# Seven products instead of eight in one more weight unit of v, with its sums of tokens formed earlier and one group's softmax scaled on ScalarE

## The chip, the cores and the metric

One core of a Trainium2 chip runs the whole program. The metric is the device time of one execution in microseconds (us), as the median of several runs; lower is better. PE stands for TensorE's matmuls, DVE for VectorE, ACT for ScalarE, POOL for GpSimd, SP for the engine that issues most transfers.

## The reference

Two layers work on 256 tokens of 2048 features. Layer 0 mixes by causal pooling, layer 1 by attention; each mixer is followed by a gated feed-forward part, with a layer norm behind every step. The change lies in layer 1. There, q, k and v are three products of the same stream with weights of 2048 x 2048, cut into 16 heads of 128:

```
k_shared = (h @ shared_w_k).reshape(B_, S, N_HEADS, HEAD_DIM)
v_shared = (h @ shared_w_v).reshape(B_, S, N_HEADS, HEAD_DIM)
...
q = (h @ w_q).reshape(B_, S, N_HEADS, HEAD_DIM)
...
s = jnp.einsum('nhbqd,nhbkd->nhbqk', qb, kw).astype(jnp.float32) * (1.0 / math.sqrt(Dh))
...
pr = jnp.exp(s - m)
den = jnp.sum(pr, axis=-1)
o = jnp.einsum('nhbqk,nhbkd->nhbqd', pr, vw.astype(jnp.float32)) / den[..., None]
```

Three dilated branches share these scores; with 256 tokens they come down to one softmax in which each key has a count of 0 to 3 (`cnt` in the kernel).

## The kernel before, in words

**Units.** All large products run over units: a unit is a block of 512 x 512 fp32 weights (1 MB). Units stand in one list, in the order in which PE works them. Every weight is split in two fp32r halves: ACT rounds the block (`wh`, L111) and DVE subtracts what was rounded off (`wl`, L112). PE then makes three products from the halves of weights and tokens. So a unit takes a transfer on SP's queue, a pass of ACT, a pass of DVE and then PE. `ahead` loads units up to 5 ahead and splits them up to 3 ahead of the one that PE is given (4 buffers for `wh` and `wl`, 3 for the raw block). There is no scheduler: each engine works its instructions in the order in which the code issues them, and `later(n, fn)` puts a piece of work behind the n-th unit from now.

**Seven products.** A unit of v is normally 24 matmuls with 512 columns (`go_t`, L265 to L267). Some units use Strassen's form: seven products of quarter size instead of eight, in 42 matmuls with 256 columns (L254 to L256). They stand in the list as two units, "a" and "b", made from one weight block. For them DVE also forms differences of weight quarters (L130, L132, L134) and splits the block in pieces (`split_sums`: ACT L129, DVE L131, and for "b" twice ACT L123 and DVE L124); and `v_sums(q)` forms sums of the tokens of quarter q: four DVE subtractions (L1093 to L1096) and, one unit later (`rest`), their two halves (ACT L1118 or L319, DVE L1120 or L315).

**Order around the change.** Heads come in four groups of four. Group 0 takes four units of k, four of q and four of v; group 1 follows with its k. I call v's units v0 to v3 and those of group 1's k next0 to next3. Before, v0, v1 and v2 are plain and v3 has seven products. Behind v1 and v2 PE makes the scores of two heads each (`scores`, L1171, L1172), and DVE and ACT then work the softmax: on DVE the mask and the maximum (L1175 to L1179), on ACT the exponentials (L1182), on DVE the counts and their sum (L1185), the reciprocal (L1187) and the scaling (L1190). `blocks` then transposes the probabilities (L1196) and moves them by transfers of SP and POOL.

Of the kernel before, what the change touches and what calls it, by code (L numbers as in the profile page):

```python
# [32 lines left out]
def trunk(ctx: ExitStack, tc: tile.TileContext, x, pool_w_in, pool_w_grp, pool_scale, pool_w_out,  # L33
# [111 lines left out]
    def later(n, fn):  # L145
        if n == 0:
            fn()
        else:
            pending.append([n, fn])
# [345 lines left out]
    def norm_evac(ps, nb, dst):  # L495
        wgb = lnp.tile([P, 4, 2], F32, name="wgb", tag="wgb", bufs=2)
        for m, n, p in pairs(ps, nb):
            A.copy(wgb[:, m:m + n, :], p[:, :n, T:XW])
        for m0, n, p in pairs(ps, nb):
            V.tensor_tensor(dst(slice(m0, m0 + n)), p[:, :n, :T], ST["rs"].to_broadcast([P, n, T]), OP.mult)  # L500
            for m in range(m0, m0 + n):
                t = dst(m)
                V.scalar_tensor_tensor(t, ST["mr"], wgb[:, m, 0:1], t, op0=OP.mult, op1=OP.subtract)
                A.activation(t, t, AF.Identity, scale=-1.0, bias=wgb[:, m, 1:2])
# [582 lines left out]
    def v_sums(q, then):  # L1087
        ap = pools["attn"]
        x = H[q]
        a11, a12, a21, a22 = (x[:, k::2, t * P:t * P + P] for k, t in ((0, 0), (1, 0), (0, 1), (1, 1)))  # L1090
        f = hp.tile([P, 4, T], F32, name="f", tag="h") if q in (0, 3) else ap.tile([P, 4, T], F32, name="f", tag="k")
        d = [f[:, i].rearrange("p (k t) -> p k t", k=2) for i in range(4)]
        V.tensor_tensor(d[0], a21, a22, OP.add)  # L1093
        V.tensor_tensor(d[1], d[0], a11, OP.subtract)
        V.tensor_tensor(d[2], a21, a11, OP.subtract)
        V.tensor_tensor(d[3], a12, d[1], OP.subtract)  # L1096

        def rest():
            if q == 0:
                u = [hp.tile([P, 4, T], F32R, name=f"xsum{hl}", tag="h") for hl in range(2)]  # L1100
                vsums[q] = [[z[:, i].rearrange("p (k t) -> p k t", k=2) for z in u] for i in range(4)]
                A.copy(u[0], f)
                V.tensor_tensor(u[1], f, u[0].bitcast(F32), OP.subtract)
                then()
                return
            if q < 3:
                t = quad_tile("xsum")
                vsums[q] = [[t[:, i, hl, :T].rearrange("p (k t) -> p k t", k=2) for hl in range(2)] for i in range(4)]
                split_act(t, f)
                then()  # L1110
                return
            w = w4("vs0").bitcast(F32R)
            z = ap.tile([P, 2, T], F32R, name="vs3", tag="vs3")
            vs = [[w[:, 0], w[:, 1]], [z[:, 0], z[:, 1]]]
            vs.append([lnp.tile([P, T], F32R, name=f"vs{nm}", tag=nm) for nm in ("S", "Q")])
            vs.append([w[:, 2], w[:, 3]])
            for i, v in enumerate(vs):
                A.copy(v[0], f[:, i])  # L1118
            for i, v in enumerate(vs):
                V.tensor_tensor(v[1], f[:, i], v[0].bitcast(F32), OP.subtract)  # L1120
            vsums[q] = [[u.rearrange("p (k t) -> p k t", k=2) for u in v] for v in vs]
            then()

        later(1, rest)

    def qk_post(nm, hq):
        def post(ps):
            later(2 if hq == 0 and nm == "k" else 0, lambda: evac(ps))

        def evac(ps):  # L1130
            ap = pools["attn"]
            o = ap.tile([P, 4, T], F32, name=nm, tag=nm)
            qk[nm] = o

            if hq == 0 and nm == "k":
                norm_evac(ps, 4, lambda m: o[:, m, :])
            else:
                for m, n, p in pairs(ps):
                    y = o[:, m:m + n, :]
                    if hq == 1 and nm == "k":  # L1140
                        A.copy(y, p[:, :, :T])
                        continue
                    A.copy(y, p[:, :, T:])
                    V.tensor_tensor(y, y, p[:, :, :T], OP.add)
            if nm == "q":
                s0, b0, b1, o0, o1 = ((2, 4, 7, 8, 11), (2, 4, 7, 12, 14), (10, 12, 15, 16, 19), (3, 4, 5, 8, 9))[hq]
                later(s0, lambda: scores(hq, range(0, 2)))
                later(b0, lambda: blocks(hq, (0, 1)))
                later(s0 + 1, lambda: scores(hq, range(2, 4)))
                if hq == 3:  # L1150
                    later(s0 + 1, lambda: blocks(hq, (2, 3)))
                else:
                    later(b1, lambda: blocks(hq, (2, 3)))
                later(o0, lambda: outputs(hq, (0, 1)))
                later(o1, lambda: outputs(hq, (2, 3)))
                if hq == 0:
                    v_sums(3, lambda: None)
                    later(6, lambda: v_sums(1, lambda: v_sums(2, lambda: None)))
                    later(11, park)
                    later(17, lambda: v_sums(0, lambda: None))  # L1160
        return post

    def scores(hq, ms):
        ap = pools["attn"]
        both = pair("s")
        two = ap.tile([P, 2, 3, P], F32, name="p", tag="p", bufs=2)
        mx = ap.tile([P, 6, 2], F32, name="mx", tag="mx", bufs=2)
        parts = ((0, slice(0, P)), (1, slice(P, 3 * P)))
        for m in ms:
            ps, q, k = both[:, m % 2, :], qk["q"][:, m, :], qk["k"][:, m, :]  # L1170
            PE.matmul(ps[:, 0:P], q[:, :P], k[:, :P], start=True, stop=True)  # L1171
            PE.matmul(ps[:, P:3 * P], q[:, P:], k, start=True, stop=True)  # L1172
        sf = two.rearrange("p h a b -> p h (a b)")
        nf, cf = (t.rearrange("p a b -> p (a b)") for t in (negm, cnt))
        V.scalar_tensor_tensor(sf, both[:, :, :3 * P], scale, nf.unsqueeze(1).to_broadcast([P, 2, 3 * P]),  # L1175
                               op0=OP.mult, op1=OP.add)
        for t, sl in parts:
            V.tensor_reduce(mx[:, t, :], sf[:, :, sl], AX.X, OP.max)
        V.tensor_scalar(mx[:, 2:4], mx[:, 0:2], -1.0, None, op0=OP.mult)  # L1179
        for h in range(2):  # L1180
            for t, sl in parts:
                A.activation(sf[:, h, sl], sf[:, h, sl], AF.Exp, bias=mx[:, 2 + t, h:h + 1])  # L1182
        for h in range(2):
            for t, sl in parts:
                V.scalar_tensor_tensor(sf[:, h, sl], sf[:, h, sl], 1.0, cf[:, sl], op0=OP.mult, op1=OP.mult,  # L1185
                                       accum_out=mx[:, 4 + t, h:h + 1])
        V.reciprocal(mx[:, 0:2], mx[:, 4:6])  # L1187
        for h in range(2):
            for t, sl in parts:
                V.tensor_scalar(sf[:, h, sl], sf[:, h, sl], mx[:, t, h:h + 1], None, op0=OP.mult)  # L1190
        pr[hq, ms[0]] = two

    def blocks(hq, ms):
        two = pr.pop((hq, ms[0]))
        b = hp.tile([P, 6 * P], F32, name="pb", tag="h")
        V.transpose(b, two.rearrange("p h s k -> p (h s k)"))  # L1196

        pool, tag = (pools["attn"], "pT") if ms[0] == 0 else (lnp, "sq")
        t = pool.tile([P, 2, 3 * P], F32, name="pTs", tag=tag)
        for m in ms:  # L1200
            pT[hq, m] = t[:, m % 2]
        to = t.rearrange("p h s -> p (h s)").rearrange("p (k a j) -> p a k j", k=6, a=4)
        fr = b.rearrange("p (k b j) -> p b k j", k=6, b=4)

        end = hq == 3 and ms[0] == 2

        def move(by, rows):
            for i in rows:
                for j in range(4):
                    by.dma_start(to[32 * j:32 * j + 32, i], fr[32 * i:32 * i + 32, j])  # L1210

        other, rows = (nc.scalar, (1,)) if end else (nc.sync, (0, 1))
        later(0 if hq == 3 else 1, lambda: move(nc.gpsimd, [i for i in range(4) if i not in rows]))
        later(1, lambda: move(other, rows))
# [21 lines left out]

    def v_group(hq):
        js = (1, 0, 3, 2) if hq == 3 else (0, 1, 2, 3)
        seven = {0: (3,), 1: (1, 2, 3), 2: js, 3: (0, 3)}[hq]
        group_tm(shared_w_v, [rows4[j] for j in js], 512 * hq, 512, [xsrcs[j] for j in js], v_post(hq),  # L1240
                 seven={i: (lambda j=j: vsums[j]) for i, j in enumerate(js) if j in seven}, early=v_early(hq))

# [157 lines left out]
```

## Time and profile before

| | |
|---|---|
| median of 3 runs | 2010.97 us (2010.79 to 2011.84) |
| profiled execution | 2010.7 us |
| its span, first to last instruction | 2008.9 us |
| PE busy | 2004.1 us (100%) |
| DVE busy | 1745.5 us (87%) |
| ACT busy | 1275.0 us (63%) |
| POOL busy | 96.4 us (5%) |
| granted TensorE clock, mean | 1.000 |

Busy time is a share of the whole span and hides that stages differ. PE's busy time includes overlap of matmuls that follow each other, so that starts of matmuls, and not their durations, tell how fast PE goes.

### The profile page before, as it was taken

What the parts mean: (1) busy time and instruction counts of PE and PEld (TensorE: products, weight loads), DVE (VectorE), ACT (ScalarE), POOL (GpSimd) and SP (SyncE); (2) the same over time, 40 slices, a digit from 0 to 9 for tenths busy, and PEclk for the clock granted to TensorE, in tenths of its full rate; (3) what the DMA queues carried; (4) which work ended last, traced back from release to release, by engine and by line L of the source; (5) the groups of instructions that cost most, each with busy time, mean ns of one, the idle gap of its engine ahead of it and who ended that gap; (6) DMA issues with size and microseconds to landing.
All of it is one profiled execution on the core that took longest, in us unless ns stands there. A gap on an engine that the chain in (4) does not pass through costs nothing.

```text
span 2008.9 us, 31723 instructions
## 1 busy us (share of the span) xinstructions
PE 2004.1 (100%) x12870; PEld 1816.1 (90%) x12870; DVE 1745.5 (87%) x1843; ACT 1275.0 (63%) x1557; POOL 96.4 (5%) x159
## 2 busy tenths in 40 slices
PE   9999999999999999999999999999999999999999
PEld 9998988999899988889898988998899989989987
DVE  6868887999899899879897878787899899989898
ACT  6455686767766676657554544577766677667673
POOL 2000000000000000000011021000000000000000
PEclk9999999999999999999999999999999999999999
DMA  8565466666566757885575657557566656665665
GB/s 278 192 210 189 168 210 189 181 226 222 191 197 207 234 185 225 233 232 185 154 244 176 213 166 230 181 189 218 161 229 196 224 188 221 197 222 190 210 217 180
DMA packets 271458, 409.89 MB, mean 204 GB/s; under 512 B 73758, under 2 KB 85492, under 8 KB 271056
## 3 DMA queue, kind: packets, MB, share of 16 engines
q1 hardware_dynamic: 257968, 388.74, 58.0%
q0 software_dynamic: 11648, 17.32, 5.6%
q8 instruction: 101, 1.65, 0.3%
q10 hardware_dynamic: 1696, 1.80, 0.3%
q14 instruction: 45, 0.37, 0.1%
HBM read 381.06 MB, written 3.15 MB: 191 GB/s over the span
## 4 chain that ended last, share of the span: by engine, by line
PE 99%; DVE 1%; issue 0%; DVEq 0%
PE acc L190 43%; PE acc L191 22%; PE s L254 3%; PE s L256 3%; PE s L255 3%; PE acc L194 3%; PE acc L193 3%; PE acc L195 3%; PE t L256 3%; PE t L254 3%; PE t L255 3%; PE t L265 1%; PE t L266 1%; PE t L267 1%; PE o L1226 0%; PE s L1172 0%
## 5 line engine op out<-in xcount | busy, mean ns | idle before, releaser
L190 PE MATMUL acc<-xc,wh 128*128 128x512 f32 x3184 | 1122.6, 395 | 0.0
L191 PE MATMUL acc<-xc,wl 128*128 128x256 f32 x3184 | 893.1, 281 | 0.0
L112 DVE TENSOR_TENSOR wl<-raw,wh 128x2048 fp32r<-128x2048 f32 (+2 forms) x302 | 650.1, 2161 | 162.6 <-ACT wh L111 157.8
L190 PEld LDWEIGHTS acc<-xc,wh 128*128 128x128 f32 x3184 | 601.0, 189 | 139.2 <-issue 0.3
L111 ACT CAST wh<-raw 128x2048 fp32r<-128x2048 f32 (+2 forms) x301 | 542.0, 1808 | 152.6 <-PE acc L190 61.6
L191 PEld LDWEIGHTS acc<-xc,wl 128*128 128x128 f32 x3184 | 600.1, 188 | 0.2
L123 ACT CAST wh<-raw 128x1024 fp32r<-128x1024 f32 x148 | 154.7, 1053 | 200.5 <-DVE raw L132 178.6
L124 DVE TENSOR_TENSOR wl<-raw,wh 128x1024 fp32r<-128x1024 f32 x148 | 176.5, 1221 | 11.2 <-ACT wh L123 11.2
L129 ACT CAST wh<-raw 128x1536 fp32r<-128x1536 f32 x74 | 109.4, 1478 | 45.9 <-PE acc L190 30.3
L131 DVE TENSOR_TENSOR wl<-raw,wh 128x1536 fp32r<-128x1536 f32 x74 | 129.7, 1753 | 9.3 <-ACT wh L129 8.4
L297 POOL DMA_DIRECT2D ht<-w x48 | 41.3, 1015 | 1437.8 <-DVE ht L954 713.8
L256 PE MATMUL t<-wh,g 128*128 128x256 f32 x376 | 105.8, 281 | 0.0
L254 PE MATMUL t<-wh,g 128*128 128x256 f32 x376 | 105.7, 281 | 0.0
L255 PE MATMUL t<-wl,g 128*128 128x256 f32 x376 | 105.4, 280 | 0.0
L697 ACT ACTIVATE c<-u,cv 128x256 f32<-128x256 f32 x172 | 89.5, 592 | 24.0 <-DVE f L759 17.3
L254 PE MATMUL s<-wh,xs 128*128 128x256 f32 x344 | 96.1, 279 | 0.0
L256 PE MATMUL s<-wh,xs 128*128 128x256 f32 x344 | 96.0, 279 | 0.0
L255 PE MATMUL s<-wl,xs 128*128 128x256 f32 x344 | 95.9, 279 | 0.0
L134 DVE TENSOR_TENSOR raw<-raw 128x1024 f32<-128x1024 f32 x74 | 90.7, 1225 | 2.5
L702 ACT ACTIVATE a<-u,cv 128x256 f32<-128x256 f32 x172 | 73.5, 499 | 11.9 <-DVE g L769 11.9
L688 ACT COPY u<-acc 128x512 f32<-128x512 f32 x84 | 46.9, 573 | 44.3 <-PE acc L191 44.1
L702 ACT ACTIVATE u<-u,cv 128x256 f32<-128x256 f32 x172 | 73.4, 498 | 0.0
(359 smaller groups left out, 3564.9 us busy)
## 6 DMA issues: line engine op xcount, KB each, us to landing
raw<-in_ffn_w_up_dram SPq DMA_DIRECT2D x160, 1024.0 KB, 5.0
raw<-in_ffn_w_down_dram SPq DMA_DIRECT2D x80, 1024.0 KB, 5.2
raw<-in_pool_w_out_dram SPq DMA_DIRECT2D x16, 1024.0 KB, 5.0
raw<-in_shared_w_k_dram SPq DMA_DIRECT2D x16, 1024.0 KB, 5.1
raw<-in_attn_w_q_dram SPq DMA_DIRECT2D x16, 1024.0 KB, 5.1
raw<-in_shared_w_v_dram SPq DMA_DIRECT2D x16, 1024.0 KB, 5.2
raw<-in_attn_w_o_dram SPq DMA_DIRECT2D x16, 1024.0 KB, 5.1
ht<-w POOLq DMA_DIRECT2D x50, 256.0 KB, 5.3
```

What stands on the lines that cost most here:

```text
L111: A.copy(wh[i][:, s], r[:, s])
L112: V.tensor_tensor(wl[i][:, s], r[:, s], wh[i][:, s].bitcast(F32), OP.subtract)
L123: A.copy(h[:, :, n], r[:, :, n])
L124: V.tensor_tensor(l[:, :, n], r[:, :, n], h[:, :, n].bitcast(F32), OP.subtract)
L129: A.copy(hs, rs)
L131: V.tensor_tensor(ls, rs, hs.bitcast(F32), OP.subtract)
L190: PE.matmul(ps[m].ap, h[:, k, c], q[:, k, :, :T], start=st, stop=False)
L191: PE.matmul(ps[m][:, :T], l[:, k, c], q[:, k, 0, :T], start=False, stop=sp)
L254: PE.matmul(to, xh, h[:, k, n], start=opens and kk == 0, stop=False)
L255: PE.matmul(to, xh, l[:, k, n], start=False, stop=False)
L256: PE.matmul(to, xl, h[:, k, n], start=False, stop=ends and kk == 1)
L702: A.activation(to[:, m, :], u[:, m, i:i + T], AF.Copy, scale=cv[:, i, j:j + 1])
```

## The change

Unit v2 of group 0 gets seven products too, so the list has one unit more, and the numbers given to `later` for group 0 behind it are raised by one; the pieces stand behind the same products as before. The sums of quarter 3 are formed behind the evacuation of k instead of that of q, those of quarter 2 behind that of q instead of after those of quarter 1, in another buffer (`hp`). For group 0 alone, the scaling of the probabilities goes from DVE to ACT, on the same data.

```diff
-        f = hp.tile([P, 4, T], F32, name="f", tag="h") if q in (0, 3) else ap.tile([P, 4, T], F32, name="f", tag="k")
+        f = hp.tile([P, 4, T], F32, name="f", tag="h") if q != 1 else ap.tile([P, 4, T], F32, name="f", tag="k")
...
             if hq == 0 and nm == "k":
                 norm_evac(ps, 4, lambda m: o[:, m, :])
+                v_sums(3, lambda: None)
...
-                s0, b0, b1, o0, o1 = ((2, 4, 7, 8, 11), (2, 4, 7, 12, 14), (10, 12, 15, 16, 19), (3, 4, 5, 8, 9))[hq]
+                s0, s1, b0, b1, o0, o1 = ((2, 4, 5, 8, 9, 12), (2, 3, 4, 7, 12, 14), (10, 11, 12, 15, 16, 19),
+                                          (3, 4, 4, 4, 8, 9))[hq]
...
-                later(s0 + 1, lambda: scores(hq, range(2, 4)))
+                later(s1, lambda: scores(hq, range(2, 4)))
...
                 if hq == 0:
-                    v_sums(3, lambda: None)
-                    later(6, lambda: v_sums(1, lambda: v_sums(2, lambda: None)))
-                    later(11, park)
-                    later(17, lambda: v_sums(0, lambda: None))
+                    v_sums(2, lambda: None)
+                    later(7, lambda: v_sums(1, lambda: None))
+                    later(12, park)
+                    later(18, lambda: v_sums(0, lambda: None))
...
-                V.tensor_scalar(sf[:, h, sl], sf[:, h, sl], mx[:, t, h:h + 1], None, op0=OP.mult)
+                if hq == 0:
+                    A.activation(sf[:, h, sl], sf[:, h, sl], AF.Copy, scale=mx[:, t, h:h + 1])
+                else:
+                    V.tensor_scalar(sf[:, h, sl], sf[:, h, sl], mx[:, t, h:h + 1], None, op0=OP.mult)
...
-        seven = {0: (3,), 1: (1, 2, 3), 2: js, 3: (0, 3)}[hq]
+        seven = {0: (2, 3), 1: (1, 2, 3), 2: js, 3: (0, 3)}[hq]
```

ACT, from the first group of exponentials to the rounding of next1. Before (`wh_9408` is next0, `wh_9462` next1):

```order
L123 CAST wh_9352<-raw_9219 128x4x256 x2
L1182 ACT_TABLE_LOAD
L1182 ACTIVATE p<-p,mx 128x128
...
L111 CAST wh_9408<-raw_9303 128x2048
L1182 ACTIVATE p<-p,mx 128x128
...
L111 CAST wh_9462<-raw_9350 128x2048
```

The same place of the change (`wh_9417` is the second half of v3, `wh_9443` next0, `wh_9497` next1):

```order
L1181 ACT_TABLE_LOAD
L1181 ACTIVATE p<-p,mx 128x128
...
L1190 ACTIVATE p<-p,mx 128x128
...
L123 CAST wh_9417<-raw_9272 128x4x256 x2
L111 CAST wh_9443<-raw_9358 128x2048
L1181 ACTIVATE p<-p,mx 128x128
...
L1190 ACTIVATE p<-p,mx 128x256
L111 CAST wh_9497<-raw_9415 128x2048
```

The rounding of v3's second half, which stood ahead of the exponentials, now stands behind them and behind four scalings; between next0 and next1 stand four exponentials and four scalings, where four exponentials stood.

DVE, from the evacuation of q to the subtraction of next1. Before (`wl_9306` and `wl_9353` are v3, `wl_9409` next0):

```order
L1144 TENSOR_TENSOR q<-q,acc 128x512 x2
...
L131 TENSOR_TENSOR wl_9306<-raw_9219,wh_9305 128x2x768
...
L124 TENSOR_TENSOR wl_9353<-raw_9219,wh_9352 128x4x256 x2
L1175 SCALAR_TENSOR_TENSOR p<-s,negm 128x768
...
L1190 TENSOR_SCALAR p<-p,mx 128x256
L112 TENSOR_TENSOR wl_9409<-raw_9303,wh_9408 128x2048
```

The same place of the change (`wl_9324` is v2's second half, `wl_9361` and `wl_9418` are v3, `wl_9444` next0, `wl_9498` next1):

```order
L124 TENSOR_TENSOR wl_9324<-raw_9166,wh_9323 128x4x256 x2
L315 TENSOR_TENSOR xsum<-f,xsum 128x4x256
...
L131 TENSOR_TENSOR wl_9361<-raw_9272,wh_9360 128x2x768
...
L1174 SCALAR_TENSOR_TENSOR p<-s,negm 128x768
...
L1186 RECIPROCAL mx<-mx 128x4
L124 TENSOR_TENSOR wl_9418<-raw_9272,wh_9417 128x4x256 x2
L112 TENSOR_TENSOR wl_9444<-raw_9358,wh_9443 128x2048
...
L112 TENSOR_TENSOR wl_9498<-raw_9415,wh_9497 128x2048
```

The first softmax now stands ahead of the second half of v3 instead of behind it, and v2's second half and the sums of quarter 2 have come in ahead of both.

## Rows read from the trace of the kernel before

**Rows 1.** The page: busy times, the chain that ended last, one transfer group

```profile
PE 2004.1 (100%) x12870; PEld 1816.1 (90%) x12870; DVE 1745.5 (87%) x1843; ACT 1275.0 (63%) x1557; POOL 96.4 (5%) x159
...
PE 99%; DVE 1%; issue 0%; DVEq 0%
...
raw<-in_shared_w_k_dram SPq DMA_DIRECT2D x16, 1024.0 KB, 5.1
```

**Rows 2.** Windows: us, busy time by engine (instructions), granted clock, DMA share, GB/s

```profile
966.00:1034.00 68.00, 68.00 (x469) 63.16 (x468) 65.52 (x94) 37.36 (x42) 10.23 (x18) 1.00 0.60 182
2005.00:2009.00 4.00, 0.40 (x2) 0.00 (x0) 0.92 (x3) 0.00 (x0) 0.00 (x0) 1.00 0.56 183
```

**Rows 3.** Timeline of PE: start, duration, line, operation; first matmuls of v1, scores, v3, next0, next1

```profile
972.74 0.39 PE L265 MATMUL t<-wh,xc 128*128 128x512 f32 x1
...
978.30 0.38 PE L1171 MATMUL s<-k,q 128*128 128x128 f32 x2
...
986.32 0.47 PE L254 MATMUL s<-wh,xc 128*128 128x256 f32 x1
...
991.39 0.28 PE L193 MATMUL acc<-xc,wh 128*128 128x256 f32 x1
...
997.09 0.28 PE L193 MATMUL acc<-xc,wh 128*128 128x256 f32 x1
...
997.32 0.27 PE L195 MATMUL acc<-xc,wl 128*128 128x256 f32 x1
```

**Rows 4.** Timeline of DVE (in brackets: idle before, and its releaser)

```profile
966.24 4.49 DVE L112 TENSOR_TENSOR wl<-raw,wh 128x2048 fp32r<-128x2048 f32 x2 [2.44 <-ACT wh L111]
970.65 1.28 DVE L1144 TENSOR_TENSOR q<-q,acc 128x512 f32<-128x512 f32 x2
971.84 0.42 DVE L1093 TENSOR_TENSOR f<-h 128x256 f32<-128x256 f32 x1
...
973.31 0.69 DVE L130 TENSOR_TENSOR raw<-raw 128x512 f32<-128x512 f32 x1
...
977.56 0.75 DVE L1120 TENSOR_TENSOR vs<-f,vs 128x256 fp32r<-128x256 f32 x2
...
978.90 2.35 DVE L124 TENSOR_TENSOR wl<-raw,wh 128x1024 fp32r<-128x1024 f32 x2
981.17 0.95 DVE L1175 SCALAR_TENSOR_TENSOR p<-s,negm 128x768 f32<-128x768 f32 x1
...
985.62 1.01 DVE L1190 TENSOR_SCALAR p<-p,mx 128x128 f32<-128x128 f32 x4
986.74 2.29 DVE L112 TENSOR_TENSOR wl<-raw,wh 128x2048 fp32r<-128x2048 f32 x1
988.95 0.95 DVE L1175 SCALAR_TENSOR_TENSOR p<-s,negm 128x768 f32<-128x768 f32 x1
...
993.39 1.01 DVE L1190 TENSOR_SCALAR p<-p,mx 128x128 f32<-128x128 f32 x4
994.51 2.29 DVE L112 TENSOR_TENSOR wl<-raw,wh 128x2048 fp32r<-128x2048 f32 x1
...
1016.92 1.22 DVE L315 TENSOR_TENSOR xsum<-f,xsum 128x1024 fp32r<-128x1024 f32 x1
```

**Rows 5.** Timeline of ACT

```profile
968.86 1.49 ACT L129 CAST wh<-raw 128x1536 fp32r<-128x1536 f32 x1
972.29 0.87 ACT L1118 CAST vs<-f 128x256 fp32r<-128x256 f32 x2 [1.94 <-DVE f L1093]
...
976.47 1.05 ACT L123 CAST wh<-raw 128x1024 fp32r<-128x1024 f32 x1 [2.64 <-DVE raw L132]
...
983.41 1.50 ACT L1182 ACTIVATE p<-p,mx 128x128 f32<-128x128 f32 x4 [3.38 <-DVE mx L1179]
984.81 1.89 ACT L111 CAST wh<-raw 128x2048 fp32r<-128x2048 f32 x1
...
992.59 3.70 ACT L111 CAST wh<-raw 128x2048 fp32r<-128x2048 f32 x2
```

More of the change, by code (lines that the diff above doesn't have):

```diff
@@ L1145, in evac @@
             if nm == "q":
-                s0, b0, b1, o0, o1 = ((2, 4, 7, 8, 11), (2, 4, 7, 12, 14), (10, 12, 15, 16, 19), (3, 4, 5, 8, 9))[hq]
+                s0, s1, b0, b1, o0, o1 = ((2, 4, 5, 8, 9, 12), (2, 3, 4, 7, 12, 14), (10, 11, 12, 15, 16, 19),
+                                          (3, 4, 4, 4, 8, 9))[hq]
                 later(s0, lambda: scores(hq, range(0, 2)))
                 later(b0, lambda: blocks(hq, (0, 1)))
-                later(s0 + 1, lambda: scores(hq, range(2, 4)))
[L1150 to L1153, printed above, removed]
+                later(s1, lambda: scores(hq, range(2, 4)))
+                later(b1, lambda: blocks(hq, (2, 3)))
                 later(o0, lambda: outputs(hq, (0, 1)))
```

## The prediction

> **What bounds the kernel now.** I read the page first. PE is busy for 2004.1 of 2008.9 us, and the chain that ended last is PE for 99% [rows 1]: whatever keeps PE waiting once is paid in full, and a shorter product is a gain only if PE need not wait for its weights. Next I read the windows over the stretch that the change touches. From 966 to 1034 us PE is busy for all 68.00 us, DVE for 65.52 and ACT for 37.36 [rows 2]. So PE sets the pace, but DVE, which must hand it the `wl` half of each unit, has 2.5 us to spare in 68. How near that is to a wait is seen when PE's timeline is laid beside DVE's. next1 is the unit to look at: DVE ends its subtraction at 994.51 + 2.29 = 996.80 [rows 4], and PE's first matmul that reads it starts at 997.32 [rows 3]. The cushion is 0.5 us, on top of a DVE that has no idle time to give.
>
> **PE's own gain.** A plain unit takes 978.30 - 972.74 = 5.56 us (v1), seven products 991.39 - 986.32 = 5.07 us (v3) [rows 3]. The change turns one into the other: 0.5 us less for PE, and it needs v2's and v3's weights the same 0.5 us sooner.
>
> **DVE's work up to the first softmax.** I lay the new order out with the durations of before, from start to start where rows follow each other. The subtraction of v1 waited for ACT until 966.24, with 2.44 us idle ahead of it; the four subtractions for quarter 3 take 973.31 - 971.84 = 1.47 us and now fit into that idle time, so v1 still starts at 966.24 [rows 4]. From there [rows 4]:
> - v1's subtraction, half of 970.65 - 966.24: 2.20, to 968.44
> - the low halves of quarter 3's sums, 978.90 - 977.56: 1.34, to 969.78
> - v2's first half (L130 to L134), 977.56 - 973.31: 4.25, to 974.03
> - the evacuation of q, 971.84 - 970.65: 1.19, to 975.22
> - quarter 2's subtractions: 1.47, to 976.69
> - v2's second half, 981.17 - 978.90: 2.27, to 978.96
> - quarter 2's low halves, the row at 1016.92: 1.22, to 980.18
> - v3's first half: 4.25, to 984.43
> - the first softmax up to its reciprocal, 985.62 - 981.17: 4.45, to 988.88.
>
> ACT keeps up so far: behind v1's rounding it has the four casts of the sums (0.87 us for two) and L129 (1.49), together 3.2 us [rows 5], and DVE gives it 2.20 + 1.34 + 0.69 = 4.2 us before it asks for L129's result. Before, DVE stood at this point at 985.62 [rows 4]. It is 3.26 us later, although the second half of v3 has been put off behind it.
>
> **What waits for the scaling.** Here the change adds a wait. The scaling is taken off DVE, where it cost 986.74 - 985.62 = 1.12 us [rows 4]. On ACT it must wait for DVE's reciprocal, and ACT works in order: behind the four scalings stand the two roundings of v3's second half, next0 and everything after. DVE's next instruction is the subtraction of just that half, so DVE waits until ACT has scaled and rounded. No row of before shows this scaling on ACT. The nearest is the exponential, on the same engine, tile, shapes and count: 984.81 - 983.41 = 1.40 us for four [rows 5]. From below, a cast with 256 columns takes 0.87 / 2 = 0.44 us [rows 5]; two of these and two with half the columns, at half of that at least, are 1.3 us. From above, I allow 1.9, a third more than the exponentials. I take 1.40, since tile, shapes and the operand per partition are the same. The Trainium skill ("ScalarE: Activation LUTs", What ACT_TABLE_LOAD costs) says that an ACTIVATE costs the same per element whatever its function, with a surcharge for an operand that is a pointer per partition. By that my estimate for the scaling (186 + 93 + 0.833 ns a column, twice 128 and twice 256 columns) is 1.76 us without overlap, the same as it gives for these exponentials, so the sum would stay. Further:
> - ACT: scaling to 988.88 + 1.40 = 990.28; the first rounding (1.05 [rows 5]) to 991.33, the second to 992.3
> - DVE idle from 988.88 to 991.33, 2.45 us; then v3's second half, 2.27, to 993.6
> - ACT: next0's rounding, half of 3.70 = 1.85 [rows 5], to 994.15; DVE waits for it 0.55 us more, then 2.20, to 996.35
> - the second softmax up to its reciprocal, 993.39 - 988.95 = 4.44 [rows 4], to 1000.79
> - ACT: scaling 1.40, then next1's rounding, 1.89 [rows 5], to 1004.08. In before that rounding ran beside DVE's scaling; now DVE waits 3.3 us
> - DVE: next1's subtraction, 2.29, to 1006.4.
>
> PE's third matmul of next1 therefore starts at about 1006.4 instead of 997.32 [rows 3]: 9.1 us later. Taken apart: 3.26 us from DVE's added work; 5.27 us from the reciprocal to next0 (988.88 to 994.15) where there were 1.12, so 4.15 more; 3.29 us from the second reciprocal to next1 where there were 1.12, so 2.17 more; less the cushion of 0.5. PE's own gain of 0.5 us is swallowed by the wait. PE pays in three places: at v3's second half (0.5 us sooner than before, v3 starts at 985.8; 18 of its 42 matmuls, 2.2 us, lead to the second half at 988.0, whose rounding comes at 991.3), at next0, and most at next1.
>
> **What doesn't count.** No transfer is late: a raw buffer for next1 is free when v2's second half is done (978.96), 5.1 us [rows 1] bring it to 984, and ACT asks for it at 1002. Behind next1 DVE has 1.47 + 1.22 = 2.7 us less than before, since quarter 2's sums are done, and PE is 9.1 us later, so the later units are no nearer to a wait than they were. The move of the probabilities starts some 9 us later, and so does the product that reads them. Nothing behind gives the time back: PE has no idle time there to lose.
>
> **The sum.** The profiled execution took 2010.7 us, 0.3 under the median of 2010.97 us. 2010.7 + 9.1 = 2019.8 us. With the scaling at 1.3 or 1.9 us, both times, it is 2019.6 or 2020.8; six hand-overs between engines at up to 0.1 us each add 0.6 at most.
>
> **Rivals.** A difference of 0.2%, some 4 us, is about what a measurement of this kernel can tell from no change.
>
> *Only DVE's work counts (no change).* If ACT had its roundings done ahead and the scaling really ran beside DVE's work, as moving it suggests, DVE at next1 would be later by 3.26, by the 2.27 of v3's second half that was put off, and earlier by the two scalings, 2.24: 3.3 us, less the cushion 2.8, so 2013.5 us. For it speaks that ACT is busy for only 37.36 of 68 us [rows 2]; against it, that its order is fixed and the roundings stand behind the scalings. The case decides on whether DVE shows the waits of 2.45 and 3.3 us.
>
> *The gain arrives (not slower).* If DVE and ACT stay ahead of PE throughout, the 0.5 us of PE's gain are left: 2010.2 us. That needs next1's `wl` by 996.8, 9.6 us before my sum has it; DVE was busy for 65.52 of 68 us, and the 2.5 us left over are less than the 3.3 us by which it is late in the rival before. It decides at next1: from 0.5 us of lateness on, PE waits. It would still read as no change: to be faster by 0.2%, eight such units would be needed.
>
> *The clock falls (slower still).* PE's waits come to about 3.3 us at v3 and some 4 us around next1. If the clock went from 2.4 to 1.2 GHz there, a unit like next1 (997.09 - 991.39 = 5.7 us [rows 3]) would take up to twice as long, 5.7 us more: 2025.5 us. What the trace has against it is the end of the span: from 2005 to 2009 PE is busy for 0.40 of 4 us, and the granted clock still reads 1.00 [rows 2], 2.4 GHz; but no work follows there that could show it. The Trainium skill ("TensorE: Matmul & The Clock Gate", HAM oscillation) says that a wait for data that is long enough throttles PE, and that the work behind it then starts cold. By that rule the 2025.5 us are the case; no run here has shown it so far.
>
> **Chances.** My forecast, a wait of about 9 us, 0.78; the clock falls as well 0.07; only DVE's work counts 0.10; the gain arrives 0.04; anything faster than that 0.01. The last three give no change or a gain: faster 0.01, no change 0.14, slower 0.85. The predicted time is 2019.8 us. The range goes from 2016.5, 3 us below the low bound of the sum, which is what remains if DVE's wait at next1 is hidden and only the one at v3 stays, to 2023.5, which takes in a clock that falls for part of a unit; outside lie the 0.15 of the three weak cases and some of the falling clock's 0.07.
>
> **What the changed profile would show.** Right, if DVE idles for some 2.5 us ahead of v3's second half and 3.3 us ahead of next1, both released by ACT's rounding, with the four scalings on ACT at about 1.4 us just ahead; if PE waits for some 3.3 us in front of v3's second half; and if the windows give 9 to 10 us of idle PE between 985 and 1010 and none behind. The sum of DVE is wrong if its first reciprocal is not near 989; the price of the scaling if its four take far from 1.4 us; the place of the wait if next1 is not the last unit that PE waits for. A granted clock under 1.00 would speak for the last rival. The forecast as a whole is wrong if PE shows no wait before 1010.

## The result, and the profile after

The changed kernel takes 2021.64 us (median of 5 runs, 2020.35 to 2023.3); the kernel before took 2010.98 us beside it (5 runs, 2010.79 to 2012.88). The ratio is 1.005, 95% interval 1.0037 to 1.0063: 10.7 us slower, against a forecast of 2019.8 us. The profiled execution of after took 2023.3 us, its span 2021.5 us, 12.6 us more than before.

Of these 12.6 us, 1.6 have nothing to do with the change. PE's matmuls stand 1.6 us later than in before from the start-up on, as here at v1, whose first matmul was at 972.74 in before [rows 3]; in another execution of the same program (`again`, below) they stand 0.1 us earlier there. Timeline of PE in after:

```profile
974.32 0.39 PE L265 MATMUL t<-wh,xc 128*128 128x512 f32 x1
...
987.29 0.47 PE L254 MATMUL s<-wh,xc 128*128 128x256 f32 x1
...
989.49 0.28 PE L256 MATMUL t<-wh,vs 128*128 128x256 f32 x1
992.88 0.38 PE L254 MATMUL s<-wh,vs 128*128 128x256 f32 x1 [3.11 <-ACT wh L123]
994.14 0.58 PE L255 MATMUL s<-wl,vs 128*128 128x256 f32 x1 [0.88 <-DVE wl L124]
...
998.48 0.28 PE L193 MATMUL acc<-xc,wh 128*128 128x256 f32 x1
...
1005.60 0.39 PE L193 MATMUL acc<-xc,wh 128*128 128x256 f32 x1 [1.26 <-ACT wh L111]
1005.82 0.28 PE L194 MATMUL acc<-xc,wh 128*128 128x256 f32 x1
1007.92 0.58 PE L195 MATMUL acc<-xc,wl 128*128 128x256 f32 x1 [1.82 <-DVE wl L112]
1008.30 0.41 PE L193 MATMUL acc<-xc,wh 128*128 128x256 f32 x1
1008.52 0.41 PE L194 MATMUL acc<-xc,wh 128*128 128x256 f32 x1
...
1011.26 0.28 PE L195 MATMUL acc<-xc,wl 128*128 128x256 f32 x1
1011.38 0.28 PE L193 MATMUL acc<-xc,wh 128*128 128x256 f32 x1
```

PE waits in two places: at v3's second half (992.88 and 994.14) and at next1 (1005.60 and 1007.92). Between them next0 starts at 998.48 without a wait. next1's third matmul, which was at 997.32 in before [rows 3], comes at 1007.92; less the 1.6 us from the start-up that is 9.0 us later. Behind it the starts of the next matmuls stand 0.21 us apart until 1011.26, and 0.12 us afterwards. 15 matmuls take 1011.26 - 1007.92 = 3.34 us where 15 x 0.119 = 1.79 are usual, another 1.6 us. That makes 10.6 of the 11.0 us; a further 0.3 us comes at 1236.90 us, where a weight load of L190 waits 0.44 us for DVE (L1233). I find a lag in this way throughout: the start of the same matmul in both kernels, behind the stretch less ahead of it.

The reason for the two waits stands in DVE's timeline of after, in brackets the idle time before and what ended it:

```profile
985.96 0.95 DVE L1174 SCALAR_TENSOR_TENSOR p<-s,negm 128x768 f32<-128x768 f32 x1
...
990.19 0.18 DVE L1186 RECIPROCAL mx<-mx 128x4 f32<-128x4 f32 x1
992.86 2.36 DVE L124 TENSOR_TENSOR wl<-raw,wh 128x1024 fp32r<-128x1024 f32 x2 [2.49 <-ACT wh L123]
995.61 2.29 DVE L112 TENSOR_TENSOR wl<-raw,wh 128x2048 fp32r<-128x2048 f32 x1 [0.39 <-ACT wh L111]
...
1002.05 0.18 DVE L1186 RECIPROCAL mx<-mx 128x4 f32<-128x4 f32 x1
1005.58 2.29 DVE L112 TENSOR_TENSOR wl<-raw,wh 128x2048 fp32r<-128x2048 f32 x1 [3.35 <-ACT wh L111]
```

and in ACT's:

```profile
990.40 1.49 ACT L1190 ACTIVATE p<-p,mx 128x128 f32<-128x128 f32 x4 [0.71 <-DVE mx L1186]
991.80 1.98 ACT L123 CAST wh<-raw 128x1024 fp32r<-128x1024 f32 x2
993.68 1.89 ACT L111 CAST wh<-raw 128x2048 fp32r<-128x2048 f32 x1
...
1002.26 1.50 ACT L1190 ACTIVATE p<-p,mx 128x128 f32<-128x128 f32 x4 [0.71 <-DVE mx L1186]
1003.66 3.68 ACT L111 CAST wh<-raw 128x2048 fp32r<-128x2048 f32 x2
```

Read them as a relay. DVE ends its reciprocal and has nothing left that it may do. ACT takes the four scalings at 990.40, and only at 991.80 the rounding; DVE goes on at 992.86, PE at 994.14. At 1002.05 the same happens for next1: reciprocal, scalings, rounding at 1003.66, subtraction at 1005.58, PE at 1007.92.

The windows of after (us, busy time of PE, PEld, DVE, ACT and POOL with instructions, granted clock, DMA share, GB/s) show where PE loses time:

```profile
966.00:1034.00 68.00, 60.92 (x396) 56.23 (x395) 58.01 (x81) 36.59 (x46) 10.23 (x18) 0.95 0.51 155
985.00:1012.00 27.00, 19.92 (x134) 19.01 (x133) 19.27 (x36) 15.31 (x23) 2.59 (x5) 0.87 0.33 113
1012.00:1034.00 22.00, 22.00 (x162) 20.82 (x161) 20.89 (x22) 10.11 (x10) 7.63 (x14) 1.00 0.90 243
```

PE was busy for 68.00 of 68 us [rows 2] and is now for 60.92; all 7.08 idle us lie between 985 and 1012, none behind. There are 9.0 us of delay at next1's third matmul but only 7.1 us idle, mainly because PE also works slower behind v3's wait: from 994.14 to 997.51 15 matmuls take 3.37 us, 1.6 more than usual, and the granted clock reads 0.75 from 995 to 1000. (PE also counts as busy up to a matmul's end, a little past the usual start of the next one, so that idle time is always somewhat less than delay.)

### The profile page after: what moved, and what is told of

Same layout as the page of the kernel before. It is cut to its first block, busy times and chain, and to the rows that moved or that the text cites. A ratio compares the mean times of both kernels' runs of the same rounds, so it can differ in the third digit from the quotient of the medians.

```text
span 2021.5 us, 31766 instructions
## 1 busy us (share of the span) xinstructions
PE 2007.9 (99%) x12888; PEld 1819.2 (90%) x12888; DVE 1748.6 (87%) x1840; ACT 1280.0 (63%) x1567; POOL 96.4 (5%) x159
## 4 chain that ended last, share of the span: by engine, by line
PE 92%; DVE 4%; DMA 2%; ACT 2%; issue 1%; SPq 0%; POOL 0%; DVEq 0%; ACTq 0%
PE acc L190 41%; PE acc L191 21%; PE s L254 3%; PE s L256 3%; PE s L255 3%; PE acc L195 3%; PE acc L194 3%; PE acc L193 3%; PE t L256 3%; PE t L254 3%; PE t L255 3%; DVE wl L112 1%; PE t L265 1%; PE t L267 1%; PE t L266 1%; ACT wh L111 1%
## 5 line engine op out<-in xcount | busy, mean ns | idle before, releaser
L190 PE MATMUL acc<-xc,wh 128*128 128x512 f32 x3184 | 1122.8, 395 | 0.0
L190 PEld LDWEIGHTS acc<-xc,wh 128*128 128x128 f32 x3184 | 600.8, 189 | 139.6 <-issue 0.3
```

Of the source, the lines that this page charges most:

```text
L190: PE.matmul(ps[m].ap, h[:, k, c], q[:, k, :, :T], start=st, stop=False)
```

## The experiments

Theory A is that of the forecast: each engine works in its fixed order, and the lateness at next1 is a sum of DVE's added work and of ACT's scalings ahead of the roundings. Its rivals are that ACT's scaling alone makes the wait (rival B), that DVE's load alone does (rival C), that it is the price of the scaling on ACT and not its place in ACT's order (rival D), and that the clock costs a large share.

**Undoing one part at a time.** Three kernels leave out one or two of the three parts (sums moved, seven products in v2, scaling on ACT). They ran with 25 runs of the kernel before, median 2011.43 us. The edits here are shown against the changed kernel.

`d_sums`, only the sums moved: v2 plain, scaling on DVE.

```diff
-                    later(7, lambda: v_sums(1, lambda: None))
+                    later(6, lambda: v_sums(1, lambda: None))
...
-                if hq == 0:
-                    A.activation(sf[:, h, sl], sf[:, h, sl], AF.Copy, scale=mx[:, t, h:h + 1])
-                else:
-                    V.tensor_scalar(sf[:, h, sl], sf[:, h, sl], mx[:, t, h:h + 1], None, op0=OP.mult)
+                V.tensor_scalar(sf[:, h, sl], sf[:, h, sl], mx[:, t, h:h + 1], None, op0=OP.mult)
...
-        seven = {0: (2, 3), 1: (1, 2, 3), 2: js, 3: (0, 3)}[hq]
+        seven = {0: (3,), 1: (1, 2, 3), 2: js, 3: (0, 3)}[hq]
```

> Only the sums move (quarter 3 behind k's evacuation, quarter 2 behind q's); v2 stays plain and the scaling stays on DVE. Theory A, each engine works in its fixed order and every us of DVE ahead of next1 beyond the cushion is paid: DVE has quarter 2's 2.69 us more ahead of next1 and uses 1.47 us of idle time, so 1.2 late less the cushion 0.5: PE waits 0.7 us at next1, about +0.7 us on 2010.98. Rival B, ACT's scaling alone makes the wait: 0. Rival C, DVE's load alone does: +0.7 as well.

Measured: 2012.12 us (2011.56 to 2012.68), ratio 1.0001 (0.9992 to 1.0011). The times alone tell nothing; the lag grows by 0.8 us in the stretch, and PE has one wait there. (In rows of waits: what PE would work, what it waited for, us in total, times, the longest.)

```profile
PE acc L195 <- DVE wl L112: 0.5, 1, 0.5
```

`c_plain`, the sums moved and the scaling on ACT, v2 plain:

```diff
-                s0, s1, b0, b1, o0, o1 = ((2, 4, 5, 8, 9, 12), (2, 3, 4, 7, 12, 14), (10, 11, 12, 15, 16, 19),
+                s0, s1, b0, b1, o0, o1 = ((2, 3, 4, 7, 8, 11), (2, 3, 4, 7, 12, 14), (10, 11, 12, 15, 16, 19),
...
-        seven = {0: (2, 3), 1: (1, 2, 3), 2: js, 3: (0, 3)}[hq]
+        seven = {0: (3,), 1: (1, 2, 3), 2: js, 3: (0, 3)}[hq]
```

> The sums move and the scaling goes to ACT; v2 stays plain. Theory A: 1.2 us from the sums, 2.2 us each from the two places where next0's and next1's rounding stand behind the scaling, less the cushion 0.5: PE waits about 5 us in front of next0 and next1, +5 us, and up to 1.5 us more if the clock falls there as it did in the changed kernel. Rival B (the scaling on ACT makes all of the wait): +9 to +10.5. Rival C (DVE's load makes it): the scaling's 2.24 us are off DVE, so 0 or less.

Measured: 2018.03 us (2017.65 to 2020.07), ratio 1.0034 (1.0021 to 1.0047). The lag is 5.1 us at next1's third matmul and 6.7 us behind the stretch. The 1.6 us between are slower matmuls, whose starts stand 0.21 us apart in next1 here too, from 1003.75 to 1006.95; the last two of these windows have clocks of 0.87 and 0.79. The rows of waits show 4.0 us, idle time alone.

```profile
PE acc L195 <- DVE wl L112: 2.5, 2, 1.8
PE acc L193 <- ACT wh L111: 1.5, 1, 1.5
...
995.00:1000.00 5.00, 3.85 (x33) 3.64 (x31) 1.56 (x9) 4.29 (x9) 0.00 (x0) 1.00 0.42 163
1000.00:1005.00 5.00, 2.81 (x16) 2.61 (x17) 4.66 (x3) 4.18 (x4) 0.83 (x2) 0.87 0.22 52
1005.00:1010.00 5.00, 5.00 (x37) 5.00 (x36) 4.90 (x7) 1.92 (x1) 3.76 (x7) 0.79 1.12 233
```

`a_dve`, the whole change, but the scaling back on DVE:

```diff
-                if hq == 0:
-                    A.activation(sf[:, h, sl], sf[:, h, sl], AF.Copy, scale=mx[:, t, h:h + 1])
-                else:
-                    V.tensor_scalar(sf[:, h, sl], sf[:, h, sl], mx[:, t, h:h + 1], None, op0=OP.mult)
+                V.tensor_scalar(sf[:, h, sl], sf[:, h, sl], mx[:, t, h:h + 1], None, op0=OP.mult)
```

> The change with its scaling put back on DVE. Theory A: first reciprocal 3.3 us late as in the changed kernel, v3's second half 2.27 us put off behind it, less the cushion 0.5: PE waits about 5 us (some 3 in front of v3's second half, 1.5 at next1), +5 us, plus up to 1.5 us for the clock, less likely here since no single wait is over 2 us. Rival B: -0.5 to +0.7. Rival C: +9 or more, since DVE has 2.24 us more than in the changed kernel.

Measured: 2016.17 us (2015.79 to 2017.49), ratio 1.0026 (1.0016 to 1.0036). The lag is 4.9 us, the clock 1.00 in every window of the stretch.

```profile
PE acc L195 <- DVE wl L112: 1.6, 2, 1.4
PE s L255 <- DVE wl L124: 1.5, 1, 1.5
PE s L254 <- ACT wh L123: 0.9, 1, 0.9
```

Without the clock's share, the four lags are 0.8 us with the sums moved and neither of the other parts, 5.1 with ACT's scaling besides, 4.9 with the seven products besides, and 9.0 with both. 5.1 + 4.9 - 0.8 = 9.2: the two parts add to within 0.2 us, as theory A has it. Either part alone makes the kernel slower, so rival B, which had `a_dve` at +0.7 at most, and rival C, which had `c_plain` at 0 or less, both fall.

**The place of the scaling, not its price.** `e_late` keeps the scaling on ACT at the same four instructions, but issues it later, just ahead of the transposition, so that no rounding stands behind it that DVE is already waiting for.

```diff
-                if hq == 0:
-                    A.activation(sf[:, h, sl], sf[:, h, sl], AF.Copy, scale=mx[:, t, h:h + 1])
-                else:
+                if hq != 0:
...
-        pr[hq, ms[0]] = two
+        pr[hq, ms[0]] = two, mx
...
-        two = pr.pop((hq, ms[0]))
+        two, mx = pr.pop((hq, ms[0]))
+        if hq == 0:
+            for h in range(2):
+                for t, sl in ((0, slice(0, P)), (1, slice(P, 3 * P))):
+                    z = two[:, h].rearrange("p a b -> p (a b)")[:, sl]
+                    A.activation(z, z, AF.Copy, scale=mx[:, t, h:h + 1])
```

> The change with ACT's scaling issued just ahead of the transposition of the probabilities, units later, so that ACT doesn't wait for the reciprocal and no rounding for next0 or next1 stands behind it; price and count of the scalings unchanged. Theory A: the two waits of 2.45 and 3.35 us on DVE go; but next0's and next1's roundings still stand behind the exponentials, and DVE has no scaling left to do meanwhile, so it waits 0.8 and 1.1 us for them: about +5 us, as with the scaling on DVE. Rival D, it is the price of the scaling on ACT and not its place: +9 or more.

Measured: 2015.97 us (2015.64 to 2017.82), ratio 1.0024 (1.0015 to 1.0034), lag 4.7 us. ACT still scales (999.52), but behind next1's rounding (997.72) instead of ahead of it. Timeline of ACT in `e_late`:

```profile
996.32 1.50 ACT L1181 ACTIVATE p<-p,mx 128x128 f32<-128x128 f32 x4 [4.48 <-DVE mx L1178]
997.72 1.89 ACT L111 CAST wh<-raw 128x2048 fp32r<-128x2048 f32 x1
999.52 1.49 ACT L1199 ACTIVATE p<-p,mx 128x128 f32<-128x128 f32 x4
```

and of DVE, at next1's subtraction, which in after had waited for 3.35 us:

```profile
999.64 2.29 DVE L112 TENSOR_TENSOR wl<-raw,wh 128x2048 fp32r<-128x2048 f32 x1 [1.15 <-ACT wh L111]
```

So it is the place of the scaling that costs over 4 us. Rival D, which had the 9 us come back whatever the place, falls. The lag that remains is about that of `a_dve`. Even in its later place the scaling is worth only 0.2 us less lag, though it takes 2.24 us off DVE: DVE then waits for ACT's roundings instead, 0.29 and 0.39 us at v3's second half and next0 and 1.15 us at next1.

**Half of the scaling.** A second series ran with 8 runs of the kernel before, median 2011.11 us. `x1_first` leaves the scaling on ACT for the first two heads of group 0 only, `x2_second` for the second two only. Here a rival B of its own has it that one of the two pairs makes all of the wait. `x1_first`:

```diff
-                if hq == 0:
+                if hq == 0 and ms[0] == 0:
```

> The change with ACT scaling for the first two heads of group 0 alone; the second pair is scaled on DVE. Theory A: the wait in front of v3's second half stays (over 3 us), that at next1 is 2.2 us shorter: +7 us. The clock falls at v3, but PE would have waited at next0 and next1 anyway, so that this costs nothing: +7.0, with little for the clock. Rival B (either scaling alone makes the wait, the other is free): +10 or +5.

`x2_second`:

```diff
-                if hq == 0:
+                if hq == 0 and ms[0] == 2:
```

> The change with ACT scaling for the second two heads of group 0 alone; the first pair is scaled on DVE. Theory A: two waits under 2 us at v3, and the whole wait of 1.4 and 2 us at next1: +7 us, and the clock's 1.5 us in full since they fall behind the last wait: +8.5. If the clock needs the long wait at v3, +7.

Measured for `x1_first`: 2018.11 us (2017.51 to 2018.43), ratio 1.0035 (1.0022 to 1.0049), lag 7.0 us. For `x2_second`: 2020.42 us (2017.79 to 2022.47), ratio 1.0047 (1.0032 to 1.0062); its profiled execution was the shortest, 2017.79 us, with a lag of 7.1 us and a clock of 1.00 behind next1. PE's waits in `x1_first` and then in `x2_second`:

```profile
PE s L254 <- ACT wh L123: 3.1, 1, 3.1
PE acc L195 <- DVE wl L112: 1.4, 1, 1.4
PE s L255 <- DVE wl L124: 0.9, 1, 0.9
```

```profile
PE acc L195 <- DVE wl L112: 1.8, 1, 1.8
PE s L255 <- DVE wl L124: 1.5, 1, 1.5
PE s L254 <- ACT wh L123: 0.9, 1, 0.9
PE acc L193 <- ACT wh L111: 0.8, 1, 0.8
```

Each pair of heads thus adds some 2.1 us to the 4.9 of `a_dve`, and neither is free. The other executions of `x2_second` were up to 4.7 us longer, at a mean clock of 0.998 instead of 0.999. The clock behind next1 may have fallen in these, but no profile of them shows it, and 1.6 us would not be enough for the longest.

**The clock.** `again` is the changed kernel once more, and `f_warm` the changed kernel with 27 extra matmuls in the waits of next1, whose results nobody reads, so that PE is not idle there.

> The changed kernel once more, to stand beside the three others on the same chip. About +10.5 us on the kernel before on this chip, as on record: 9 of wait and 1.5 of clock.

```diff
+            def idle(count):
+                for _ in range(count):
+                    PE.matmul(ps[0][:, T:], XC[0][:, 0, 0, :P], XC[0][:, 0, 0, :T], start=False, stop=False)
+
+            if fill:
+                idle(fill[0])
...
+                    if fill and i == 0:
+                        idle(fill[1])
...
+              mode="x" if x0 else "a" if hq == 1 else "ab", fill=(11, 16) if hq == 1 else None)
```

> The changed kernel with 27 extra matmuls in next1 (11 ahead of its first product, 16 ahead of the first one that reads wl), on data that is there, into PSUM columns that nobody reads: PE has work during the 1.4 and 2.0 us in which it waits. Theory A with the clock as a term of its own (1.5 us): the granted clock doesn't fall behind next1's wait, and the kernel is 1.5 us faster than the changed one, some +9 us on the kernel before, though it does more work. If the slow matmuls after the wait have another reason (the data, the write port), nothing is gained: +10.5 or up to 0.5 more.

Measured for `again`: 2020.83 us (2019.84 to 2021.73), ratio 1.0049 (1.0034 to 1.0064), so 9.7 us slower. In its profiled execution (2019.92 us) the third matmul of next1 comes at 1006.26, with the start-up taken off 9.0 us late as in after, but the matmuls behind follow at 0.12 us. The windows of `again` and then of after around next1 differ in the clock:

```profile
990.00:995.00 5.00, 3.11 (x13) 2.82 (x14) 3.42 (x3) 3.91 (x4) 0.00 (x0) 0.61 0.07 7
995.00:1000.00 5.00, 5.00 (x33) 5.00 (x33) 4.32 (x12) 1.49 (x4) 0.00 (x0) 0.71 1.00 368
1000.00:1005.00 5.00, 4.09 (x33) 3.67 (x31) 1.61 (x4) 4.41 (x6) 0.00 (x0) 1.00 0.12 45
1005.00:1010.00 5.00, 3.74 (x31) 3.74 (x32) 4.96 (x5) 2.76 (x3) 2.25 (x4) 1.00 0.51 161
```

```profile
995.00:1000.00 5.00, 5.00 (x34) 5.00 (x34) 4.54 (x6) 0.57 (x1) 0.00 (x0) 0.75 0.74 238
1000.00:1005.00 5.00, 4.33 (x37) 4.13 (x35) 1.58 (x10) 4.23 (x9) 0.00 (x0) 1.00 0.48 182
1005.00:1010.00 5.00, 2.58 (x11) 2.38 (x12) 4.42 (x3) 4.41 (x4) 0.59 (x1) 0.78 0.15 36
```

The same program has a lag of 9.1 us in one execution and of 10.6 in the other, and the clock behind next1 is the difference. DVE's waits are the same in both (2.49, 0.39 and 3.36 us in `again`), but PE's are not: in `again` the clock stays down for longer behind v3 (0.61 and 0.71), PE is done with next0 0.9 us later and so idles for 0.4 and 1.8 us at next1, where after has 1.3 and 1.8. Whether that is why the clock stayed up there is not shown. Behind v3 the lower clock costs nothing in either: PE is through with v3 and next0 sooner than next1's weights are there, even so, and next1's third matmul is 9.0 us late both times.

`f_warm` took 2021.4 us (2020.09 to 2022.02), ratio 1.0052 (1.0035 to 1.0068), and not the 1.5 us less that was expected; the interval of its ratio holds that of `again`, 1.0049. In its profile PE shows no wait at next1 and the clock reads 1.00 from 1000 us on. But the clock does so in `again` too, without the extra matmuls, and these delay next1's third matmul by some 0.4 us (lag 9.5). This test says nothing on whether they keep the clock up. Nor can the medians of four runs: from one profile to another PE's matmuls stand 0.2 us earlier to 1.6 us later than in before from the start-up on, as much as the term that was looked for.

## Why the prediction was right

- **DVE's work up to the first softmax.** Forecast 988.88 for the end of the first reciprocal; ACT's scaling, which waits for it, starts at 990.40, and less the start-up's 1.59 that is 988.81.
- **The scaling on ACT.** Forecast 1.40 us for four from the exponential's row; from their start to the rounding's it is 991.80 - 990.40 = 1.40, and 1.40 again at 1002.26, so the row's price held. My estimate from the Trainium skill ("ScalarE: Activation LUTs", What ACT_TABLE_LOAD costs) was 1.76 us without overlap; with the overlap of some 93 ns that the same section gives for ACTIVATEs back to back, the estimate is 1.48 us. The trace agrees: the four are busy for 1.49 us.
- **DVE's waits.** Forecast 2.45, 0.55 and 3.3 us, measured 2.49, 0.39 and 3.35. The hand-overs between engines, allowed for at up to 0.1 us, are shorter: the first reciprocal ends at 990.37 and the scaling starts at 990.40.
- **PE.** Forecast 9.1 us at next1's third matmul, measured 9.0. The wait at v3 was forecast at 3.3 us and shows as 3.1 + 0.9; the 0.9, for DVE's half of the same weights, was left out. The wait at next0, the second of the three named, is not there: behind v3's wait PE is late itself, and slower. Mainly for the same reason the sign of 9 to 10 us of idle PE between 985 and 1010 was not met: it is 7.1 us.
- **The three terms taken apart.** The added work (3.26) and v3's second half put off (2.27) less the cushion (0.5) make 5.0 us; `a_dve`, which has just these, shows 4.9. The rest of the first term of ACT is 4.15 - 2.27 = 1.9, where `x1_first` adds 2.1; the second is 2.17, where `x2_second` adds 2.2.
- **PE's own gain** of 0.5 us is there at v3, whose first matmul comes 0.6 us sooner (987.29 - 1.59 = 985.70, before 986.32 [rows 3]), and is swallowed by the wait just behind, as said; `a_dve`, with seven products and no scaling on ACT, is 4.7 us slower than before.
- **Rivals.** "Only DVE's work counts" falls with DVE's waits of 2.49 and 3.35 us. "The gain arrives" falls with the waits of PE: no kernel here is faster than before.
- **The clock, the term that was mis-sized.** The forecast had no clock in the sum and gave it 0.07, at a price of 5.7 us. It falls in both profiles of the changed kernel, and every run of it has a mean of 0.997 or 0.998 (so has the profile of `again`, which lost nothing by it, so that the mean doesn't tell what a run paid). But behind next1 it is at the lower level for 15 matmuls and not for a unit, so that there it costs 1.6 us, or nothing, from one execution to the next; behind v3 it costs nothing, since the next wait hides it. With 0 to 1.6 us added, 2019.8 becomes 2019.8 to 2021.4; the medians were 2021.64, just above that, and 2020.83. What I read at the end of the span, where no work followed, was no evidence on this. The rule in the Trainium skill ("TensorE: Matmul & The Clock Gate", HAM oscillation), that a wait for data can throttle PE and the work behind it starts cold, agrees with after's 0.21 us between starts behind v3's wait of 3.1 us and behind next1's; in `again` it holds at v3, while the work behind next1's waits of 0.4 and 1.8 us did not start cold (0.12 us).

The two parts, seven products and the scaling on ACT, cost 4 us each where they stand, and what they could give at PE is 0.5 us.

## What to carry to other kernels

When work is moved to an engine that has idle time, look at what stands behind it in that engine's order: a move to ACT that saves DVE 1.12 us made DVE wait for 2.5 and 3.35 us, because the next thing that ACT does is what DVE needs. Each of the two moves made the kernel some 2.1 us slower than with that scaling on DVE (`x1_first` and `x2_second` against `a_dve`). Such a forecast can be made with the durations of before, laid out instruction by instruction in the new order; here it met each of DVE's three waits to 0.2 us. A shorter product was worth nothing here, where the engine that prepares its operands was full (65.5 of 68 us).

## What was not expected of the hardware

- The granted clock behind PE's waits differs between executions of the same program: 0.78 and 1.00 in the 5 us around next1, with DVE's waits the same and PE's not quite (1.3 and 1.8 us against 0.4 and 1.8). Where it falls, starts of matmuls go from 0.12 to 0.21 us apart, near the two levels of 2.4 and 1.2 GHz.
- The length of the waits doesn't tell whether it falls. `a_dve` and `x2_second` do the same work up to next0 and both waited 0.9 and 1.5 us at v3: `a_dve` kept 1.00 and `x2_second` had 0.72. With waits of 0.9 and 0.9 us at the same place `e_late` had 0.66. What decides it stays open. Windows from 990 to 995 us, of `a_dve`, of `x2_second` and of `e_late`:

```profile
990.00:995.00 5.00, 3.71 (x29) 3.50 (x29) 5.00 (x4) 1.90 (x2) 0.00 (x0) 1.00 0.26 78
```

```profile
990.00:995.00 5.00, 4.16 (x25) 4.16 (x26) 4.99 (x4) 1.62 (x1) 0.00 (x0) 0.72 0.34 110
```

```profile
990.00:995.00 5.00, 4.60 (x26) 4.60 (x27) 4.62 (x4) 1.84 (x2) 0.00 (x0) 0.66 0.46 139
```
